# Top-k search in sparse attention: one of two streams of tiles is bisected on ScalarE with sign sums

## The chip, the cores and the metric

One core of one Trainium2 chip. The metric is the device time of one execution in microseconds.

## The reference

Two blocks of a network run one after the other on a sequence of 1024 rows of 1024 features, all in float32. The first block has two layers. In each, a normed and modulated input is projected; one half goes through a spatial gating unit, the other through sparse attention: for every query row an index score against all earlier keys is formed, the 256 best keys are kept, and only these take part in the softmax.

```python
logits = jnp.einsum('bthd,bsd->bths', qib, k_idx) * (IDX_DIM ** -0.5)
score = jnp.einsum('bth,bths->bts', wb, jax.nn.relu(logits)).astype(jnp.float32)
score = jnp.where(causal[None], score, -jnp.inf)
_, idx = lax.top_k(score, top)                     # top = 256
valid = idx <= qpos[None, :, None]
k_sel, v_sel = gather(k, idx), gather(v, idx)
sc = jnp.einsum('bthd,btkd->bthk', qb, k_sel) * attn_scale
p = jax.nn.softmax(jnp.where(valid[:, :, None, :], sc, -jnp.inf), axis=-1)
return jnp.einsum('bthk,btkd->bthd', p, v_sel)
```

The second block has one layer with windowed attention, a gated convolution and a mixture of 32 experts. The change does not touch it.

## The kernel before

The sequence is cut into 8 tiles of 128 rows (tile 0 to tile 7). Rows 0 to 255 keep all their keys, so only tiles 2 to 7 search. Tile i has n = 128 (i + 1) keys.

The search finds, for every one of a tile's 128 rows (one row a partition), the value of the 256th best score. It works on the upper 16 bits of the float scores as signed integers, `up` (L646). One count over `up` says on which side of zero the threshold lies (L648). From it follow `pos`, the rank `K` that is looked for, and the first candidate (L650 to L657). Then a loop of 15 bits (L659 to L666) halves the interval: count how many values reach the candidate (`count`, L605 to L608, one VectorE instruction over n elements with an accumulator output, which the profile shows as TENSOR_SCALAR_CACHE_REDUCE and a DVE_READ_ACCUMULATOR), compare with K (L662, `xb`), move the candidate (L664, `cand`). What the count writes out beside its sum, `junk`, is never read. After the loop `lower` (L690, L695) and `choose` (L702 to L721) take the lower 16 bits and ties into account and write the mask `bias` of the tile.

`select(i)` is a Python generator that does this for tile i: it turns the queries (L544), scores them on TensorE (L629), ScalarE (L632, `rel`) and VectorE (L635, L637), masks the future on GpSimd (L640), searches and chooses. Two streams run interleaved (L762): stream 0 takes tiles 2, 4 and 6, stream 1 tiles 3, 5 and 7 (`z = i % 2` names their small tiles). Each `yield` gives the stream's cost on VectorE and a delay in ns; `bg` and `resume` (L191 to L216) are a planner that emits the next step of the stream that is due first, against a clock of modelled TensorE time, so that the search is interleaved with the dense products. The framework then orders the instructions of each engine by priority with a timing model of its own (`schedule_with_timeline_sim`).

Around the search, in the order of emission: the products of v, u, q, z_a and z_b (`dense_nat`, `dense_T1`; weights arrive as `wraw`, ScalarE makes `whi` at L108, GpSimd `wlo` at L111). The silu of z_b is ScalarE's tanh at L949 and VectorE's L950. L465 and L471 are VectorE's modulation rows, L816 its spatial gating, L507 its part of transposes. `recheck` (L724 to L755) is a branch of VectorE and the DMA queue for rows with many ties; behind it attention (`front`, `back`: L854 to L896) may use the masks, those of tiles 2 to 5 after the second feature block of z_b, those of 6 and 7 later. Attention's Exp is L858 on ScalarE, after VectorE's row maxima (`mx`, L855).

Of the kernel before, what the change touches and what calls it, by code (L numbers as in the profile page):

```python
# [10 lines left out]
FT = mybir.dt.float32  # L11
FR = mybir.dt.float32r
BF = mybir.dt.bfloat16
# [2 lines left out]
U32 = mybir.dt.uint32  # L16
U16 = mybir.dt.uint16
F16 = mybir.dt.float16
AF = mybir.ActivationFunctionType
OP = mybir.AluOpType  # L20
AX = mybir.AxisListType
# [3 lines left out]
S = 1024  # L25
# [15 lines left out]
def tile_hybrid(ctx, tc, I, out):  # L41
    nc = tc.nc
    V, A, G, T = nc.vector, nc.scalar, nc.gpsimd, nc.tensor
# [31 lines left out]
    mhalf = const.tile([128, 16], FT, name="mhalf")  # L75
# [28 lines left out]
    def split(hi, lo, src, which="pool", sub=None):  # L104
        if which == "pool":
            G.tensor_scalar(hi, src, 1.0, 0.0, op0=OP.mult, op1=OP.add)
        elif which == "act":
            A.activation(hi, src, AF.Copy)  # L108
        else:
# [171 lines left out]
    def rms_tile(x, dst, g, scr):  # L281
        ss = small.tile([128, 1], FT, name="ss", bufs=8)
        A.activation(scr, x, AF.Square, accum_out=ss)
        ms = small.tile([128, 1], FT, name="ms", bufs=8)
# [29 lines left out]
    small1 = b1.enter_context(tc.tile_pool(name="small1", bufs=3))  # L314
# [3 lines left out]
    tmp = b1.enter_context(tc.tile_pool(name="tmp", bufs=2))  # L318
# [7 lines left out]
    def rope_tables(after):  # L326
# [14 lines left out]
        for which, q in ((sinT, 0.0), (cosT, 0.25)):  # L341
# [7 lines left out]
            V.tensor_scalar(r, r, -3.1415925, 3.1415925, op0=OP.max, op1=OP.min)  # L349
            A.activation(which, r, AF.Sin)  # L350

# [3 lines left out]
    def silu_c(c8):  # L355
        cc = bank([128, NT], "sm")
        T.transpose(cc, c8, ident[0:NT, 0:NT])
        th = small1.tile([128, NT], FT, name="cct", bufs=1)
        A.activation(th, cc, AF.Tanh, scale=0.5)
        V.scalar_tensor_tensor(th, th, 1.0, cc, op0=OP.add, op1=OP.mult)  # L360
# [12 lines left out]
    def first_h(hT):  # L373
# [8 lines left out]
        def products(c, n, e):  # L382
# [3 lines left out]
            for part in (1, 0):  # L386
# [18 lines left out]
                if e[part] == "m":  # L405
                    A.activation(acc[0:1], pr, AF.Copy)
            return c, n, e, accs

        def use(c, n, e, accs):
# [7 lines left out]
            for cc in range(c, c + n):  # L417
                for b in range(2):
                    ps = bank([128, 4, 128], "tr")
                    for j in range(4):  # L420
# [3 lines left out]
                    y = tmp.tile([128, 512], FT, name="yT", tag="r2", bufs=7)  # L424
                    A.activation(hT[0][:, cc, ts], pv, AF.Identity, scale=mcol[:, 1, cc:cc + 1],
                                 bias=mcol[:, 0, cc:cc + 1])
# [132 lines left out]
    def layer(l, xin, hT=None):  # L559
# [39 lines left out]
        bias, bias_, kept = {}, {}, {}  # L599
        fl = small1.tile([128, 6], BF, name="fl", bufs=1)  # L600
        scd = dram.tile([128, 6, S], FT, name=f"scd{l}")
        junk = tmp.tile([128, S], BF, name="junk", tag="r2", bufs=7)
        headed, scored = set(), set()

        def count(src, thr, op, z):  # L605
            cnt = small1.tile([128, 1], FT, name=f"cnt{z}")
            V.tensor_scalar(junk[:, :src.shape[1]], src, thr, 0.0, op0=op, op1=OP.add, accum_out=cnt)  # L607
            return cnt  # L608

        def select(i):  # L610

            z = i % 2
            n = 128 * (i + 1)
# [31 lines left out]
            up = tmp.tile([128, n], I16, name="up", tag="r2", bufs=7)  # L645
            V.tensor_copy(up, sc.bitcast(I16)[:, 1:2 * n:2])  # L646
            yield 100.0 + .55 * n, False, 0.0, 0.0
            cnt = count(up, 0.0, OP.is_ge, z)  # L648
            pos = small1.tile([128, 1], FT, name=f"pos{z}", bufs=1)
            V.tensor_scalar(pos, cnt, 256.0, None, op0=OP.is_ge)  # L650
            few = small1.tile([128, 1], FT, name=f"few{z}", bufs=1)
# [1 line left out]
            K = small1.tile([128, 1], FT, name=f"K{z}", bufs=1)  # L653
            V.tensor_scalar(K, pos, float(256 - (n - 255)), float(n - 255), op0=OP.mult, op1=OP.add)
            V.tensor_tensor(K, K, few, op=OP.add)
            cand = small1.tile([128, 1], FT, name=f"cand{z}")
            V.tensor_scalar(cand, pos, 32768.0, -16384.0, op0=OP.mult, op1=OP.add)  # L657
            yield 700.0 + .52 * n, False, 0.0, 0.0
            for b in range(14, -1, -1):  # L659
                x = small1.tile([128, 1], FT, name=f"xb{z}")  # L660
                cnt = count(up, cand[:, 0:1], OP.is_ge, z)
                V.tensor_scalar(x, cnt, K[:, 0:1], -float(2 ** b), op0=OP.is_lt, op1=OP.mult)  # L662
                c2 = small1.tile([128, 1], FT, name=f"cand{z}")
                V.scalar_tensor_tensor(c2, x, 2.0 ** (b - 1) if b else 0.0, cand, op0=OP.add, op1=OP.add)  # L664
                cand = c2
                yield 360.0 + .52 * n, False, 0.0, 0.0  # L666

# [30 lines left out]
        def choose(sc, gt, c, cand, z, eq=None, pre=None):  # L698
# [13 lines left out]
            if eq is None:  # L712
                eq = tmp.tile([128, n], BF, name="eq", tag="r2", bufs=7)
                pre = tmp.tile([128, n], F16, name="pre", tag="r2", bufs=7)
            V.tensor_scalar(eq, sc, thr[:, 0:1], None, op0=OP.is_equal)
# [8 lines left out]
        def recheck(tiles):  # L724
# [14 lines left out]
            for arm in tc.Switch({DVE: many, SP: many}, 2):  # L739
                if arm == 1:  # L740
                    for i in tiles:
                        n = 128 * (i + 1)
                        sc, cand = sct[:, :n], kept[i][:, 1:2]
                        up, lw = wt[0][:, 0, :n], wt[0][:, 1, :n].bitcast(U16)
                        eq, pre = wt[1][:, 0, :n].bitcast(BF), wt[1][:, 1, :n].bitcast(F16)
                        nc.sync.dma_start(sc, scd[:, i - 2, :n])
# [10 lines left out]
        def stream(tiles):  # L757
            for i in tiles:
                yield from select(i)
# [331 lines left out]
    hT0 = [big.tile([128, 8, S], FR, name="s32") for _ in range(2)]  # L1091
    rope_tables(first_h(hT0))
    x1 = layer(0, x0, hT0)
    x2 = layer(1, x1)
    b1.close()

# [239 lines left out]
    def gate():  # L1336
        sg = sgpool.tile([128, 2, S], FT, name="sg", tag="sg")

        def ev_g(f, h, ps):
            A.activation(sg[:, f, h * 512:(h + 1) * 512], ps, AF.Tanh, scale=0.5)  # L1340
        dense_T(8, rhs, ev_g)
        return sg
# [3 lines left out]
    sg = gate()  # L1346
# [3 lines left out]
    for br, src in enumerate((convf, attnf)):  # L1350
# [4 lines left out]
        for dc in range(4):  # L1355
            if br or dc:
                sg = gate()
# [58 lines left out]
    pos = keep2.tile([128, NT, 2], FT, name="pos")  # L1416
# [149 lines left out]
    cnt = keep2.tile([128, NE], FT, name="cnt")  # L1566
# [207 lines left out]
```

## Time and profile before

| | us |
|---|---|
| median of 3 runs (lowest, highest) | 2437.85 (2428.63, 2440.24) |
| profiled execution | 2434.67 |
| its span, first to last instruction | 2432.7 |
| first layer's search, first count to attention of tile 2 | about 156 to 503 in the span |
| second layer's search | about 835 to 1160 in the span |

The page gives busy times of the engines (PE is TensorE, DVE VectorE, ACT ScalarE, POOL GpSimd) and cuts the span into 40 slices of 60.8 us; the views below cut it more finely.

### The profile page before, as it was taken

The numbers are of one execution on the slowest core, as the hardware profiler recorded it, in microseconds if no ns is written. First come the engines' busy times: TensorE is split into PE (matmuls) and PEld (weight loads), VectorE is DVE, ScalarE is ACT, GpSimd is POOL, SyncE is SP. The second block draws the span as 40 slices with busy tenths as digits, with TensorE's granted clock in tenths as the row PEclk, the third lists the DMA queues.
The fourth block names the chain that finished last, engine by engine and source line by source line (L and its number), as shares of the span: only waits on it lengthen the run. The fifth ranks groups of instructions, "written<-read, shape, count | busy, mean of one in ns | idle before, by whom it ended". The sixth has DMA issues, their size and how long they took to land. (4 is left out here: it accounts for less than half of the span.)

```text
span 2432.7 us, 36229 instructions
## 1 busy us (share of the span) xinstructions
PE 2165.2 (89%) x13235; PEld 1895.6 (78%) x13235; DVE 1649.2 (68%) x3539; ACT 1065.5 (44%) x1907; POOL 1081.0 (44%) x1006
## 2 busy tenths in 40 slices
PE   5998898699989979986999899999999897899996
PEld 5897786577779978964878698888888676888875
DVE  8779898977774688897778427872010335798875
ACT  4333333455642333334646335652121212678775
POOL 4654465447745652745455245533233512232221
PEclk9999999789999989987999999999999998999998
DMA  7522112311114111123120211113121164999995
GB/s 233 186 80 82 47 31 77 97 61 58 53 38 135 48 36 47 41 72 96 49 84 23 52 44 36 31 31 81 48 64 45 50 238 165 305 346 336 333 335 153
DMA packets 146508, 265.50 MB, mean 109 GB/s; under 512 B 23672, under 2 KB 100880, under 8 KB 134016
## 3 DMA queue, kind: packets, MB, share of 16 engines
q1 hardware_dynamic: 139136, 241.99, 30.2%
q0 software_dynamic: 7168, 20.98, 4.0%
q8 instruction: 105, 1.72, 0.3%
q14 instruction: 99, 0.81, 0.1%
HBM read 228.83 MB, written 38.29 MB: 110 GB/s over the span
## 5 line engine op out<-in xcount | busy, mean ns | idle before, releaser
L111 POOL TENSOR_TENSOR wlo<-wraw,whi 128x512 fp32r<-128x512 f32 (+1 forms) x188 | 253.6, 1350 | 490.3 <-ACT whi L108 472.8
L101 PE MATMUL big<-wlo,s 128*128 128x256 f32 (+1 forms) x1536 | 440.0, 288 | 11.0 <-POOL wlo L111 11.0
L100 PE MATMUL big<-whi,s 128*128 128x256 f32 (+1 forms) x1536 | 437.8, 289 | 11.7 <-ACT s L506 9.3
L102 PE MATMUL big<-whi,s 128*128 128x256 f32 (+1 forms) x1536 | 440.1, 288 | 0.0
L101 PEld LDWEIGHTS big<-wlo,s 128*128 128x128 f32 x1536 | 298.7, 195 | 16.1 <-POOL wlo L111 13.4
L100 PEld LDWEIGHTS big<-whi,s 128*128 128x128 f32 x1536 | 296.2, 194 | 19.1 <-ACT s L506 11.9
L108 ACT ACTIVATE whi<-wraw 128x512 fp32r<-128x512 f32 (+1 forms) x188 | 117.8, 628 | 417.4 <-PE big L102 140.9
L102 PEld LDWEIGHTS big<-whi,s 128*128 128x128 f32 x1536 | 298.2, 194 | 2.9 <-issue 0.9
L111 DVE TENSOR_TENSOR ew<-s,ew 128x1024 fp32r<-128x1024 f32 x138 | 162.8, 1221 | 35.0 <-ACT ew L108 33.7
L607 DVE TENSOR_SCALAR_CACHE_REDUCE junk<-up,cand 128x512 bf16<-128x512 int16 (+5 forms) x192 | 179.8, 937 | 1.4
L637 DVE SCALAR_TENSOR_TENSOR s<-rel,widx,s 128x384 f32<-128x384 f32 (+3 forms) x140 | 130.5, 956 | 51.0 <-ACT rel L632 50.5
L632 ACT ACTIVATE rel<-sm 128x384 f32<-128x384 f32 (+3 forms) x160 | 80.9, 524 | 161.9 <-PE sm L629 104.4
L100 PE MATMUL half<-s,whi 128*128 128x512 f32 x320 | 133.1, 417 | 18.0 <-DVE s L950 14.7
L108 ACT ACTIVATE ew<-s 128x1024 fp32r<-128x1024 f32 x138 | 137.8, 1049 | 25.3 <-PE sm L102 16.3
L100 PE MATMUL sm<-ew,xT 128*96 128x256 f32 x512 | 146.6, 286 | 2.0 <-ACT xT L1621 2.0
L102 PE MATMUL sm<-ew,xT 128*96 128x256 f32 x512 | 147.3, 288 | 0.6 <-DVE xT L1622 0.6
L101 PE MATMUL sm<-ew,xT 128*96 128x256 f32 x512 | 145.3, 284 | 0.8 <-DVE ew L111 0.7
L101 PE MATMUL half<-s,whi 128*128 128x512 f32 x320 | 131.2, 410 | 0.0
L102 PE MATMUL half<-s,wlo 128*128 128x512 f32 x320 | 129.8, 409 | 0.3 <-POOL wlo L111 0.3
L1659 POOL DMA_INDIRECT out_dram<-yt,yi x32 | 60.1, 1878 | 149.9 <-DMA out_dram<-yt,yi 86.5
L862 POOL TENSOR_SCALAR Z<-Z,rc 128x128 f32<-128x128 f32 (+7 forms) x88 | 63.4, 733 | 108.9 <-DVE rc L860 66.4
L629 PE MATMUL sm<-kist,qT 128*128 128x384 f32 (+3 forms) x320 | 91.2, 376 | 14.4 <-ACT rel L632 13.0
(624 smaller groups left out, 6118.0 us busy)
## 6 DMA issues: line engine op xcount, KB each, us to landing
wraw<-in_w_in_dram SPq DMA_DIRECT2D x164, 256.0 KB
adaw<-in_w_ada_dram SPq DMA_DIRECT2D x48, 512.0 KB
s<-in_w_gate_e_dram SPq DMA_DIRECT2D x23, 1024.0 KB
s<-in_w_up_e_dram SPq DMA_DIRECT2D x23, 1024.0 KB
s<-in_w_down_e_dram SPq DMA_DIRECT2D x23, 1024.0 KB
X<-in_w_gate_e_dram SPq DMA_DIRECT2D x9, 1024.0 KB
X<-in_w_up_e_dram SPq DMA_DIRECT2D x9, 1024.0 KB
X<-in_w_down_e_dram SPq DMA_DIRECT2D x9, 1024.0 KB
```

Source lines behind the costliest of these rows:

```text
L100: T.matmul(o, lh, rh, start=start, stop=False, skip_group_check=True)
L101: T.matmul(o, lh, rl, start=False, stop=False, skip_group_check=True)
L102: T.matmul(o, ll, rh, start=False, stop=stop, skip_group_check=True)
L108: A.activation(hi, src, AF.Copy)
L111: return (sub or V).tensor_tensor(lo, src, hi.bitcast(FT), op=OP.subtract)
L607: V.tensor_scalar(junk[:, :src.shape[1]], src, thr, 0.0, op0=op, op1=OP.add, accum_out=cnt)
L629: T.matmul(ps[:, :w_], qT[g][:, j, :], kist[a][:, p * w_:(p + 1) * w_], start=a == 0, stop=a == 1)
L632: A.activation(rel[:, :w_], ps[:, :w_], AF.Relu, scale=0.125)
L637: V.scalar_tensor_tensor(d, rel[:, :w_], widx[:, i, h:h + 1], d, op0=OP.mult, op1=OP.add)
L862: G.tensor_scalar(P[hh][:, :n], P[hh][:, :n], rc[:, hh:hh + 1], 1.0, op0=OP.mult, op1=OP.mult)
L1659: return G.indirect_dma_start(out=out, out_offset=bass.IndirectOffsetOnAxis(ap=ycol, axis=0), in_=yt, in_offset=None, bounds_check=S + SL ...
```

## The change

For tiles 3, 5 and 7 the first count and the 15 bits move from VectorE to ScalarE. A count becomes one activation, Sign(up - candidate + 0.5), with an accumulator output: its sum is (number above) minus (number below). A second Sign over one column says whether the count reaches K, and an Identity over one column moves the (negated) candidate. A few scalings of one column around the loop stay on VectorE. These steps charge the planner no VectorE time and a delay of 800 + 0.85 n ns a bit. For tiles 2, 4 and 6 the candidate's move (L664) becomes a tensor_scalar with the old candidate as a per-partition scalar. `junk` becomes two halves of 8-bit integers in the same bytes, one for VectorE's counts and one for ScalarE's.

```diff
--- before.py
+++ after.py
@@ -16,6 +16,7 @@
 U32 = mybir.dt.uint32
 U16 = mybir.dt.uint16
 F16 = mybir.dt.float16
+I8 = mybir.dt.int8
 AF = mybir.ActivationFunctionType
 OP = mybir.AluOpType
 AX = mybir.AxisListType
@@ -599,8 +600,36 @@
         bias, bias_, kept = {}, {}, {}
         fl = small1.tile([128, 6], BF, name="fl", bufs=1)
         scd = dram.tile([128, 6, S], FT, name=f"scd{l}")
-        junk = tmp.tile([128, S], BF, name="junk", tag="r2", bufs=7)
+        junk8 = tmp.tile([128, 2, S], I8, name="junk", tag="r2", bufs=7)
+        junk = junk8[:, 0]
         headed, scored = set(), set()
+
+        junk2 = junk8[:, 1]
+
+        def count_act(up, off, scale=1.0):
+
+            sg = small1.tile([128, 1], FT, name="xb1")
+            A.activation(junk2[:, :up.shape[1]], up, AF.Sign, bias=off, scale=scale, accum_out=sg)
+            return sg
+
+        def bisect_act(up, K, pos, n):
+
+            kb = small1.tile([128, 1], FT, name="few1", bufs=1)
+            V.tensor_scalar(kb, K, -2.0, float(n + 1), op0=OP.mult, op1=OP.add)
+            nc_ = small1.tile([128, 1], FT, name="cand1")
+            V.tensor_scalar(nc_, pos, -32768.0, 16384.5, op0=OP.mult, op1=OP.add)
+            for b in range(14, -1, -1):
+                sg = count_act(up, nc_[:, 0:1])
+                s_ = small1.tile([128, 1], FT, name="cnt1")
+                A.activation(s_, sg, AF.Sign, bias=kb[:, 0:1])
+                if b:
+                    n2 = small1.tile([128, 1], FT, name="cand1")
+                    A.activation(n2, s_, AF.Identity, scale=-2.0 ** (b - 1), bias=nc_[:, 0:1])
+                    nc_ = n2
+                yield 0.0, False, 800.0 + .85 * n, 0.0
+            cand = small1.tile([128, 1], FT, name="cand1")
+            V.tensor_scalar(cand, s_, 0.5, nc_[:, 0:1], op0=OP.mult, op1=OP.subtract)
+            return cand
 
         def count(src, thr, op, z):
             cnt = small1.tile([128, 1], FT, name=f"cnt{z}")
@@ -645,7 +674,12 @@
             up = tmp.tile([128, n], I16, name="up", tag="r2", bufs=7)
             V.tensor_copy(up, sc.bitcast(I16)[:, 1:2 * n:2])
             yield 100.0 + .55 * n, False, 0.0, 0.0
-            cnt = count(up, 0.0, OP.is_ge, z)
+            if z:
+                sg = count_act(up, mhalf[:, 0:1], -1.0)
+                cnt = small1.tile([128, 1], FT, name=f"cnt{z}")
+                V.tensor_scalar(cnt, sg, -0.5, 0.5 * n, op0=OP.mult, op1=OP.add)
+            else:
+                cnt = count(up, 0.0, OP.is_ge, z)
             pos = small1.tile([128, 1], FT, name=f"pos{z}", bufs=1)
             V.tensor_scalar(pos, cnt, 256.0, None, op0=OP.is_ge)
             few = small1.tile([128, 1], FT, name=f"few{z}", bufs=1)
@@ -653,15 +687,18 @@
             K = small1.tile([128, 1], FT, name=f"K{z}", bufs=1)
             V.tensor_scalar(K, pos, float(256 - (n - 255)), float(n - 255), op0=OP.mult, op1=OP.add)
             V.tensor_tensor(K, K, few, op=OP.add)
-            cand = small1.tile([128, 1], FT, name=f"cand{z}")
-            V.tensor_scalar(cand, pos, 32768.0, -16384.0, op0=OP.mult, op1=OP.add)
-            yield 700.0 + .52 * n, False, 0.0, 0.0
-            for b in range(14, -1, -1):
+            if not z:
+                cand = small1.tile([128, 1], FT, name=f"cand{z}")
+                V.tensor_scalar(cand, pos, 32768.0, -16384.0, op0=OP.mult, op1=OP.add)
+            yield 700.0 + (0.0 if z else .52 * n), False, 0.0, 0.0
+            if z:
+                cand = yield from bisect_act(up, K, pos, n)
+            for b in () if z else range(14, -1, -1):
                 x = small1.tile([128, 1], FT, name=f"xb{z}")
                 cnt = count(up, cand[:, 0:1], OP.is_ge, z)
                 V.tensor_scalar(x, cnt, K[:, 0:1], -float(2 ** b), op0=OP.is_lt, op1=OP.mult)
                 c2 = small1.tile([128, 1], FT, name=f"cand{z}")
-                V.scalar_tensor_tensor(c2, x, 2.0 ** (b - 1) if b else 0.0, cand, op0=OP.add, op1=OP.add)
+                V.tensor_scalar(c2, x, 2.0 ** (b - 1) if b else 0.0, cand[:, 0:1], op0=OP.add, op1=OP.add)
                 cand = c2
                 yield 360.0 + .52 * n, False, 0.0, 0.0
 
```

## Rows read from the trace of the kernel before

**Rows 1.** The page: busy time, share of the span and instructions of each engine, and the 40 slices of TensorE and VectorE in tenths.
```profile
PE 2165.2 (89%) x13235; PEld 1895.6 (78%) x13235; DVE 1649.2 (68%) x3539; ACT 1065.5 (44%) x1907; POOL 1081.0 (44%) x1006
...
PE   5998898699989979986999899999999897899996
...
DVE  8779898977774688897778427872010335798875
```

**Rows 2.** Busy time of each engine in stretches of the two searches (stretch in us from the start of the span: its length, then the busy time and instructions of TensorE, its weight loads, VectorE, ScalarE and GpSimd; then the granted TensorE clock as a share of full speed, the DMA share and GB/s). Six stretches for each layer: tiles 2 and 3 bisected, between, tiles 4 and 5, between, tiles 6 and 7, the tail.
```profile
156.00:216.00 60.00, 55.36 (x444) 52.98 (x442) 59.14 (x205) 17.61 (x29) 15.33 (x12) 1.00 0.37 105
216.00:270.00 54.00, 44.49 (x278) 40.71 (x279) 46.43 (x56) 19.66 (x41) 35.82 (x23) 0.81 0.23 64
270.00:345.00 75.00, 64.22 (x467) 59.91 (x466) 73.34 (x199) 20.33 (x38) 32.81 (x35) 0.98 0.16 42
345.00:384.00 39.00, 35.14 (x247) 33.25 (x247) 30.23 (x38) 17.94 (x33) 36.13 (x35) 0.96 0.14 40
384.00:456.00 72.00, 59.89 (x263) 47.92 (x261) 70.57 (x185) 24.24 (x56) 23.16 (x28) 0.91 0.25 77
456.00:503.00 47.00, 24.34 (x93) 17.64 (x91) 38.12 (x88) 24.31 (x57) 30.08 (x28) 0.60 0.29 91
835.00:893.00 58.00, 44.27 (x328) 42.72 (x327) 57.67 (x192) 20.07 (x36) 32.84 (x25) 0.85 0.12 36
893.00:938.00 45.00, 45.00 (x356) 44.91 (x357) 29.67 (x64) 19.87 (x41) 8.27 (x7) 1.00 0.18 50
938.00:993.00 55.00, 50.07 (x381) 48.06 (x380) 54.38 (x153) 14.07 (x25) 31.37 (x33) 1.00 0.15 42
993.00:1040.00 47.00, 42.94 (x298) 40.99 (x297) 37.70 (x63) 19.96 (x35) 34.70 (x35) 0.93 0.14 39
1040.00:1115.00 75.00, 63.72 (x292) 50.69 (x290) 73.10 (x183) 24.45 (x59) 24.98 (x30) 0.91 0.24 74
1115.00:1160.00 45.00, 21.75 (x87) 16.68 (x86) 30.63 (x74) 25.07 (x56) 28.66 (x28) 0.62 0.34 101
```

**Rows 3.** Who TensorE waited for from 156 to 503 us, longest in total first (instruction and line that waited, who released it: us in total, times, longest).
```profile
PE half L100 <- DVE s L950: 11.3, 3, 6.8
PE sm L629 <- ACT rel L632: 8.0, 6, 3.5
PE sm L854 <- DVE qT L544: 5.5, 1, 5.5
PE tr L538 <- DVE wml L507: 5.3, 1, 5.3
PE sm L469 <- DVE ada L465: 5.1, 1, 5.1
...
PE sm L100 <- DVE bt L471: 2.4, 1, 2.4
...
PE sm L100 <- DVE xb L662: 2.0, 2, 1.7
```

**Rows 4.** Groups of VectorE instructions from 156 to 503 us, shapes kept apart (line, operation, tiles, shapes, count; busy us, mean ns of one; idle before).
```profile
L664 DVE SCALAR_TENSOR_TENSOR cand<-xb,cand 128x1 f32<-128x1 f32 x90 | 26.8, 298 | 0.5
L607 DVE TENSOR_SCALAR_CACHE_REDUCE junk<-up,cand 128x1024 bf16<-128x1024 int16 x16 | 20.3, 1271 | 0.1
...
L662 DVE TENSOR_SCALAR xb<-cnt,K 128x1 f32<-128x1 f32 x90 | 18.6, 207 | 0.3
...
L607 DVE TENSOR_SCALAR_CACHE_REDUCE junk<-up,cand 128x768 bf16<-128x768 int16 x16 | 16.0, 1001 | 0.0
...
L607 DVE TENSOR_SCALAR_CACHE_REDUCE junk<-up,cand 128x512 bf16<-128x512 int16 x16 | 11.7, 733 | 0.0
...
L607 DVE DVE_READ_ACCUMULATOR junk<-up,cand 128x1 f32 x96 | 7.8, 81 | 0.0
```

**Rows 5.** Groups of ScalarE instructions of the whole span, shapes kept apart: the Exp of attention with a pointer bias and an accumulator output, its accumulator read, a two-column activation without pointers, and the table loads ahead of Silu (L936) and Exp (L858).
```profile
L858 ACT ACTIVATION_READ_ACCUMULATOR Z<-Z,mx 128x1 f32 x88 | 16.6, 189 | 0.0
...
L858 ACT ACTIVATE Z<-Z,mx 128x1024 f32<-128x1024 f32 x8 | 9.2, 1153 | 1.9 <-DVE mx L855 1.9
...
L858 ACT ACTIVATE Z<-Z,mx 128x768 f32<-128x768 f32 x8 | 7.4, 930 | 2.9 <-DVE mx L855 2.9
...
L858 ACT ACTIVATE Z<-Z,mx 128x128 f32<-128x128 f32 x16 | 6.4, 399 | 42.6 <-DVE mx L855 42.6
L1229 ACT ACTIVATE mx<-mx 128x2 f32<-128x2 f32 x32 | 6.3, 195 | 8.3 <-DVE mx L1228 8.1
...
L858 ACT ACTIVATE Z<-Z,mx 128x512 f32<-128x512 f32 x8 | 5.7, 717 | 0.3 <-DVE mx L855 0.3
...
L936 ACT ACT_TABLE_LOAD x2 | 2.6, 1283 | 0.0
L858 ACT ACT_TABLE_LOAD x2 | 2.6, 1283 | 0.0
```

**Rows 6.** VectorE in order of time: the first and the last count of tile 7 in the first layer (start us, us, engine, line, operation).
```profile
412.36 1.27 DVE L607 TENSOR_SCALAR_CACHE_REDUCE junk<-up,cand 128x1024 bf16<-128x1024 int16 x1
...
464.84 1.28 DVE L607 TENSOR_SCALAR_CACHE_REDUCE junk<-up,cand 128x1024 bf16<-128x1024 int16 x1
```

**Rows 7.** Who ScalarE waited for from 156 to 503 us: the row of the Exp.
```profile
ACT Z L858 <- DVE mx L855: 32.1, 12, 7.7
```

**Rows 8.** TensorE in order of time: one matmul of z_b at 1.2 GHz, and one of the same shape at 2.4 GHz (start us, us).
```profile
409.33 0.63 PE L102 MATMUL half<-s,wlo 128*128 128x512 f32 x1
...
415.86 0.40 PE L102 MATMUL half<-s,wlo 128*128 128x512 f32 x1
```

## Prediction

> **What bounds the kernel now.** I read the page first: TensorE is busy 89% of the span and VectorE 68%, ScalarE only 44% [rows 1]. By the averages TensorE is the bound. The slices say where it is not: VectorE's row of tenths stands at 7 to 9 while the two top-k searches run, and TensorE's row dips to 6 at the end of each [rows 1]. So next I cut the two search stages into stretches [rows 2]. In the first layer VectorE is busy 59.1 of 60, 73.3 of 75 and 70.6 of 72 us in the three stretches where tiles 2 and 3, 4 and 5, 6 and 7 are bisected, and the second layer repeats this (57.7 of 58, 54.4 of 55, 73.1 of 75). There VectorE is full, and TensorE loses time. Over the six stretches of the first layer TensorE is busy 283.4 of 347 us, so it idles 63.6; over those of the second 267.8 of 325, 57.2 idle.
>
> The waits of TensorE say for whom it idles: for a VectorE result that stands in VectorE's queue among the counts. L950 (the silu of z_b) costs 11.3 us, L507 5.3, L465 5.1, L471 2.4, L662 2.0 [rows 3], together 26.1; another 8.0 is ScalarE's rel of the scoring. The tails (456 to 503 and 1115 to 1160, when the last tile's mask is made and the attention of tiles 2 and 3 starts) hold 22.7 and 23.3 us of idle TensorE [rows 2]. Last, the granted clock is 0.60 and 0.62 in the tails and 0.81 to 1.00 elsewhere [rows 2]: idle TensorE also falls from 2.4 to 1.2 GHz, where one matmul takes 0.63 instead of 0.40 us [rows 8].
>
> **The change part by part.** *VectorE, removed for tiles 3, 5, 7.* Per layer 16 counts a tile go (one for the sign, 15 bits): 16 x (0.733 + 1.001 + 1.271) = 48.1 us; 48 accumulator reads at 0.081 = 3.9; 45 of L662 at 0.207 = 9.3; 45 of L664 at 0.298 = 13.4 [rows 4]. That is 74.7. Added are four small scalings a tile (cnt, kb, the first and the last cand) against the one cand that goes: 9 x 0.207 = 1.9.
>
> *VectorE, tiles 2, 4, 6.* L664 turns from a form with two tensor inputs into one with one tensor and a per-partition scalar, the form of L662. Mean 298 against 207 ns [rows 4]: 45 x 0.091 = 4.1 us a layer saved. Bounds: nothing, and 10 us, were the form as short as the accumulator read (81 ns). The count now writes 8-bit junk. No row shows that output; the counts cost 1.05 ns an element ((1271 - 733) / 512 [rows 4]). I take nothing; were it twice as slow per element, the 45 counts left would cost some 38 us a layer more and half of the relief would be gone. Net relief taken: 77 us a layer, of 318 and 283 that VectorE is busy in the two stages [rows 2].
>
> *ScalarE, added.* One bit is a Sign over n elements with a pointer bias and an accumulator read, a Sign of one column and an Identity of one column. The nearest row to the first is the Exp of the attention, which also has a pointer bias and an accumulator: 717, 930 and 1153 ns for 512, 768 and 1024 columns, and 189 for the read [rows 5]. A column of one lies between L1229 (195 ns, no pointer) and the 128-column Exp (399 ns) [rows 5]; taking 0.85 ns a column off the latter ((1153 - 717) / 512) leaves 290, which I use. A bit is then 1.49, 1.69, 1.92 us, a tile 22, 25, 29 us, with the first counts 80 us a layer (bounds 71 and 89). ScalarE goes from 124 to 204 of 347 us in the first stage: not a bound.
>
> The Trainium skill speaks against this: "ScalarE: Activation LUTs", section Rules for kernel authors, wants simple elementwise work on VectorE, which it puts at up to three times as fast. By that a 1024-column count would take 3.8 us on ScalarE and tile 7's chain nearly 70 us. The trace disagrees for this operation: 1271 ns on VectorE [rows 4], 1153 on ScalarE [rows 5].
>
> *The chain of tile 7.* Its 15 bits and the last count stand from 412.4 to 466.1 on VectorE [rows 6], 53.7 us, though one bit by itself is 1.27 + 0.08 + 0.21 + 0.16 = 1.7 us: the rest is other work in the queue. On ScalarE the bits are 29 us; ScalarE is busy 24.2 of 72 us there [rows 2], so stretched by 1 / (1 - 0.34) the chain takes 44, and it starts earlier since VectorE scores sooner. Tile 6 keeps VectorE to itself at the same time. What is late next: the z_b products, which keep TensorE until 456, and then the branch of recheck, which VectorE takes only behind the masks that stand in front of it.
>
> *The queues.* No transfer is moved. Instructions behind a Sign on ScalarE wait up to 1.2 us: the rel of the scoring, the whi halves of the weights, the evacuations, all of which TensorE waits for. There are 254 ScalarE instructions in the stage [rows 2], and the new work holds ScalarE 80 / 347 = 23% of it. Half a count, 0.47 us, x 0.23 x 254 = 27 us a layer if each were on TensorE's path; double buffers cover most, as rel ends only 8.0 us of TensorE's idle time now [rows 3]. I take a quarter, 7 us. The planner's yields change too: stream 1 charges VectorE nothing and is paced by 800 + 0.85 n ns a bit, about what I get above for a bit (1.24 to 1.67 against 1.49 to 1.92), so the search is emitted no later.
>
> *Sum.* (a) Of the 26.1 us of VectorE-ended waits outside the tail two thirds go, since VectorE falls from full to about 60%: 17; the second layer by its idle time (57.2 / 63.6): 16. (b) The tails are chains of latency, but begin earlier and with z_b products still to fill TensorE: half, 11 + 12. (c) Clock: busy time x (1 - clock) over the stretches of [rows 2] is 26 + 24 us lost to 1.2 GHz; a third comes back with the idle time, 16. (d) ScalarE's queue: -14. Together 58 us. The profiled execution took 2434.67 us (span 2432.7), so 2377; it lies 3 us under the median of the runs, so I say 2378.
>
> **The rivals.** *The tail stays.* The masks are ready sooner, but the branch and the first attention units set the tail (the wait on L544 behind the branch is 5.5 us [rows 3]). Then (b) is nothing and (c) half: 33 + 8 - 14 = 27, 2410. For it: that longest wait of the tail stands behind the branch, not behind a count. Against: tile 7's last count ends at 466 [rows 6], inside the tail.
>
> *The wait moves to ScalarE.* All 27 us a layer of (d) count: 58 + 14 - 54 = 18 faster; if the tail stays too, 2435 to 2440. No change. For it: ScalarE feeds TensorE with everything. Against: it is 34% busy in that stretch.
>
> *Slower: the bits stand behind Exps.* ScalarE runs in order, and the Exps of the first attention units wait 32.1 us for VectorE's maxima in the first stage [rows 7]. A bit queued behind such an Exp waits with it. With all of it in tile 7's chain it takes 29 + 18 + 32 = 79 us against 53.7 now: the tail comes 25 us later in each layer, 2435 + 50 - 33 + 14 = 2466. It decides once over 7 us of these waits fall between bits and VectorE's relief shortens none of them; but the maxima wait in the very queue that is relieved.
>
> *Slower: function tables.* Loads of 1.283 us stand ahead of the first Silu and the first Exp of a layer [rows 5]; Relu, Copy and Identity bring none. If Sign were not in the table of Exp, every turn from a bit to an Exp and back would cost 2.6 us; with 15 turns in tile 7's chain 38 us a layer, the end 28 us later: 2435 + 56 - 33 = 2458. Beside this stands the Trainium skill, "ScalarE: Activation LUTs", section Table sets: it wants calls grouped by table set, and lists cheap functions as part of every set without naming Sign in that list; no row here shows Sign.
>
> **How the numbers follow.** Forecast 0.62 (its own range 2330 to 2410); the tail stays 0.15; the wait moves to ScalarE 0.10; behind Exps 0.09; tables 0.04. The first two are faster: 0.77. The third is the same: 0.10. The last two are slower: 0.13. About 0.5%, 12 us, is what the runs can tell from no change. The low end takes all of (a), the whole of both tails and half of (c), without (d): 50 + 46 + 25 = 121, 2314; I cut it to 2322. The high end, 2440, takes in the unchanged case and leaves out the two slower ones.
>
> **What would show it.** Right: VectorE's busy time down by some 150 us and ScalarE's up by some 160; a Sign of 1024 columns near 1.15 us; VectorE at 60 to 75% in the six stretches; the L950, L507 and L465 waits nearly gone; tails at a higher clock; no more table loads than before. Wrong: counts with 8-bit output above 1.3 us for 896 columns; new waits of TensorE on ScalarE above 20 us a layer; bits more than 3 us apart with an Exp waiting between them; the end of tile 7's search no earlier relative to the z_b products.

## The result: 0.8% slower

The changed kernel takes 2456.2 us (median; 2447.1 to 2460.6) against 2437.8 for the kernel before: a ratio of 1.0078, 95% interval 1.0062 to 1.0094. I had forecast 2378, with a range of 2322 to 2440, and given slower a chance of 0.13.

The page of the changed kernel (busy time, and the rows of TensorE, VectorE and ScalarE in 40 slices), against [rows 1]:

```profile
PE 2175.8 (89%) x13235; PEld 1898.2 (77%) x13235; DVE 1532.6 (62%) x3185; ACT 1199.9 (49%) x2273; POOL 1063.6 (43%) x1006
...
PE   5999598689988988985999899999999888899986
...
DVE  8677967377864587763868517873010234798875
ACT  4355362854642464538546424663121111778774
```

The work moved as meant: VectorE is 117 us less busy and ScalarE 134 more, TensorE's work is the same 13235 matmuls (10.6 us longer busy). Yet TensorE's row falls to 5 where it stood at 8 in the fifth slice (246 to 307 us, in the first search), and to 5 where it stood at 6 in the nineteenth (1105 to 1167 us, the end of the second).

To place the loss I cut each layer at three events that every kernel here has: the first `up` of the search, the start of the last tanh of z_b (L949, here L986), and the first use of an output projection (L1028, here L1065). Between the first two lies what I call the head, in which the search runs beside dense products; between the last two the tail, in which the search ends and attention begins. The same view as [rows 2], for the kernel before (head, tail, head, tail):

```profile
156.80:457.80 301.00, 258.95 (x1689) 234.36 (x1687) 281.04 (x683) 100.80 (x198) 144.17 (x131) 0.93 0.23 67
457.80:518.30 60.50, 37.68 (x160) 28.00 (x161) 48.68 (x114) 34.81 (x81) 34.08 (x35) 0.69 0.33 106
829.80:1118.50 288.70, 251.79 (x1688) 232.58 (x1686) 260.19 (x679) 103.24 (x205) 133.75 (x131) 0.93 0.18 51
1118.50:1173.00 54.50, 34.06 (x153) 26.62 (x154) 38.37 (x93) 32.56 (x75) 32.75 (x35) 0.69 0.36 112
```

And for the changed kernel:

```profile
160.20:450.70 290.50, 251.90 (x1658) 226.15 (x1656) 220.48 (x494) 142.60 (x317) 137.32 (x126) 0.92 0.23 69
450.70:529.70 79.00, 47.26 (x193) 36.84 (x193) 46.41 (x124) 58.83 (x145) 33.17 (x42) 0.61 0.26 83
844.80:1116.70 271.90, 244.94 (x1649) 226.47 (x1647) 202.66 (x468) 143.48 (x315) 130.60 (x124) 0.93 0.19 55
1116.70:1197.00 80.30, 46.21 (x193) 34.20 (x193) 46.07 (x124) 60.03 (x149) 33.07 (x42) 0.66 0.23 75
```

The heads gain 10.5 and 16.8 us, the tails lose 18.5 and 25.8; 3.4 us more are lost ahead of the first head and 3.6 between the layers, and the rest of the span shifts by the sum, 24. About half of a tail's loss (9.6 and 12.2 us of TensorE's busy time) is products that now run there (193 matmuls where there were 160 and 153), at a granted clock of 0.61 and 0.66 where it was 0.69; the rest is idle TensorE.

In the tail tile 7's bits are now a chain on ScalarE. The Signs of its 15 bits (the line's instructions from 430 to 500 us; durations min/median/max, first and last start), and VectorE's wait for the last of them:

```profile
L612 ACT ACTIVATE junk<-up,cand x15: 1132/1147/1150, 440.5 to 491.1; 128x1024 int8<-128x1024 int16 x15
```
```profile
DVE cand L631 <- ACT cnt L624: 5.4, 1, 5.4
```

TensorE's waits from 156 to 530 us (who waited, for whom: total, times, longest):

```profile
PE sm L101 <- DVE e L713: 14.0, 1, 14.0
PE sm L891 <- DVE mx L892: 12.1, 2, 11.0
PE sm L658 <- ACT rel L661: 9.7, 7, 2.7
...
PE half L101 <- DVE s L987: 5.0, 1, 5.0
```

The z_b wait of [rows 3] fell from 11.3 to 5.0 us, the way that was forecast, but the longest is new, and the second has more than doubled. In the kernel before, the same stretch had for it:

```profile
PE sm L854 <- DVE mx L855: 5.2, 4, 2.4
```

That wait, for attention's first maxima (L892, before L855), is the tail's; the 14.0 us belong to the head. VectorE in that stretch (start, duration):

```profile
285.81 0.21 DVE L699 TENSOR_SCALAR xb<-cnt,K 128x1 f32<-128x1 f32 x1
286.06 0.21 DVE L701 TENSOR_SCALAR cand<-xb,cand 128x1 f32<-128x1 f32 x1
286.31 0.88 DVE L636 TENSOR_SCALAR_CACHE_REDUCE junk<-up,cand 128x640 int8<-128x640 int16 x1
...
295.59 0.75 DVE L853 SCALAR_TENSOR_TENSOR X<-sm,bs,X 128x512 f32<-128x512 f32 x1
296.26 0.22 DVE L713 SCALAR_TENSOR_TENSOR e<-rank,K,m 128x8 f32<-128x8 f32 x1
```
```profile
296.49 0.77 PE L101 MATMUL sm<-vs,wmh 128*128 128x512 f32 x1 [13.96 <-DVE e L713]
```

From 279 to 291 us VectorE does nothing but the bits of tile 4, one every 1.42 us. L853, which empties the `sm` bank that the spatial gating's next products need, stands behind them and behind four more us of tile 4's next steps and tile 5's scoring. (The profile names `e`, L713, which ends 0.14 us after L853, as the releaser.) In the kernel before the bits of tiles 4 and 5 alternate at this place and the same instruction (L816 there) is let in between:

```profile
291.57 0.86 DVE L607 TENSOR_SCALAR_CACHE_REDUCE junk<-up,cand 128x640 bf16<-128x640 int16 x1
...
292.44 0.74 DVE L816 SCALAR_TENSOR_TENSOR X<-sm,bs,X 128x512 f32<-128x512 f32 x1
...
293.22 1.00 DVE L607 TENSOR_SCALAR_CACHE_REDUCE junk<-up,cand 128x768 bf16<-128x768 int16 x1
```

### The profile page after: what moved, and what is told of

It reads as the page before. It is cut to its first block, busy times and chain, and to the rows that moved or that the text cites. A ratio compares the mean times of both kernels' runs of the same rounds, so it can differ in the third digit from the quotient of the medians.

```text
span 2456.2 us, 36272 instructions
## 1 busy us (share of the span) xinstructions
PE 2175.8 (89%) x13235; PEld 1898.2 (77%) x13235; DVE 1532.6 (62%) x3185; ACT 1199.9 (49%) x2273; POOL 1063.6 (43%) x1006
## 5 line engine op out<-in xcount | busy, mean ns | idle before, releaser
L102 PEld LDWEIGHTS big<-wlo,s 128*128 128x128 f32 x1536 | 295.5, 193 | 19.0 <-POOL wlo L112 16.8
L101 PEld LDWEIGHTS big<-whi,s 128*128 128x128 f32 x1536 | 292.8, 192 | 20.4 <-ACT s L507 11.0
L103 PEld LDWEIGHTS big<-whi,s 128*128 128x128 f32 x1536 | 295.4, 193 | 1.2
L666 DVE SCALAR_TENSOR_TENSOR s<-rel,widx,s 128x384 f32<-128x384 f32 (+3 forms) x140 | 118.4, 867 | 91.5 <-ACT rel L661 91.2
L1696 POOL DMA_INDIRECT out_dram<-yt,yi x32 | 53.5, 1673 | 131.7 <-DMA out_dram<-yt,yi 43.8
L101 PE MATMUL big<-s,whi 128*128 128x512 f32 x256 | 101.2, 395 | 0.3 <-DVE convf L1349 0.3
L102 PE MATMUL big<-s,whi 128*128 128x512 f32 x256 | 101.1, 395 | 0.0
```

The costliest lines, as they stand in the source:

```text
L101: T.matmul(o, lh, rh, start=start, stop=False, skip_group_check=True)
L102: T.matmul(o, lh, rl, start=False, stop=False, skip_group_check=True)
L103: T.matmul(o, ll, rh, start=False, stop=stop, skip_group_check=True)
L666: V.scalar_tensor_tensor(d, rel[:, :w_], widx[:, i, h:h + 1], d, op0=OP.mult, op1=OP.add)
L1696: return G.indirect_dma_start(out=out, out_offset=bass.IndirectOffsetOnAxis(ap=ycol, axis=0), in_=yt, in_offset=None, bounds_check=S + SL ...
```

## The experiments

Three theories were set against each other. A: tile 7's bits are one long serial chain on a busy ScalarE at the end of the search. B, later called D: bits on ScalarE disturb its other work, whatever the tile. C: the planner's pace changed the order of emission, and the loss is one of order. Each kernel was timed in five rounds beside the kernel before, whose median lay at 2436 to 2438 us.

**The scalar form alone.** The kernel before, with

```
- V.scalar_tensor_tensor(c2, x, 2.0 ** (b - 1) if b else 0.0, cand, op0=OP.add, op1=OP.add)
+ V.tensor_scalar(c2, x, 2.0 ** (b - 1) if b else 0.0, cand[:, 0:1], op0=OP.add, op1=OP.add)
```

> One part alone: the kernel before, with the candidate's move of all six tiles in the form with a per-partition scalar, and nothing on ScalarE. All theories of the loss lie in the ScalarE search, so all expect no loss here. By the rows of the two traces (298 ns before, 0.207 us for such a form) VectorE is relieved by 90 x 0.091 = 8 us a layer, on a VectorE that is full there: 2422 to 2438 us. If the loss came from this part, the time would be 2445 or more.

2416.8 us, ratio 0.9926 (0.9912 to 0.9940): 19 us faster, below the 2422 to 2438 that were expected. The loss is not here; the rest of the change (the bits on ScalarE, their pace, the 8-bit `junk`) costs 39 us on top of this. L664 over the whole span, before and in this kernel:

```profile
L664 DVE SCALAR_TENSOR_TENSOR cand<-xb,cand 128x1 f32<-128x1 f32 x180 | 60.6, 337 | 1.6
```
```profile
L664 DVE TENSOR_SCALAR cand<-xb,cand 128x1 f32<-128x1 f32 x180 | 37.7, 210 | 1.5
```

**Which tiles.** In the changed kernel the condition `if z` became `if i in (3, 5)`, and in a second kernel `if i in (7,)`; the other tiles stay on VectorE in the scalar form.

> The changed kernel with tile 7 back on VectorE; only tiles 3 and 5 are bisected on ScalarE. Theory A (the long pole: tile 7's bits end late because they are one serial chain on a ScalarE that other work fills at the end of the search): the tail's loss of 18 to 26 us a layer goes and the 10 to 15 us gained ahead of it stay, so 2405 to 2425 us, and the wait of TensorE for the first attention's maxima (12.1 and 12.6 us) shrinks. Theory B (any ScalarE bits disturb the evacuations, whichever tile they belong to): two thirds of the loss stay, about 2450 us. Theory C (the planner emits stream 1 too late): tile 5's delay still pushes tile 7 back, so its first count comes later than 412 us and the time stays at 2440 or more.

> Only tile 7 is bisected on ScalarE, tiles 3 and 5 on VectorE. Theory A: the relief ahead of the tail is missing, and the tail is as in the changed kernel or a little better, as tile 7 starts earlier than with tile 5 in its stream on ScalarE: 2445 to 2475 us. Theory B: a third of the bits, a third of the loss: about 2444 us. Theory C: tile 7's scoring begins about when it did before (up at 408 us), so the tail is as long as before and the time is 2438 us or less.

Tiles 3 and 5: 2443.1 us, ratio 1.0027 (1.0015 to 1.0039), 26 above the scalar form alone. Tile 7: 2419.4 us, 0.9926 (0.9911 to 0.9941), the same within noise. These times are the reverse of theory A: with tile 7 back on VectorE most of the loss stays, and tile 7 alone costs next to nothing. B, which asked for 2444, doesn't fit tile 7's figure either. Theory C has both times right, but not tile 7's tail: it was to be as long as before, and it is 82 and 83 us against 59 and 53 in the scalar form. The heads are 25 and 29 us shorter, so that the sum comes out at nothing (table below).

**The planner's delay of a bit.** From 800 + 0.85 n ns to half, to 0.7 and to a quarter of it:

```
- yield 0.0, False, 800.0 + .85 * n, 0.0
+ yield 0.0, False, 400.0 + .42 * n, 0.0      (0.7: 560.0 + .6 * n; a quarter: 200.0 + .21 * n)
```

> The changed kernel with half the planner's delay a bit (400 + 0.42 n ns in place of 800 + 0.85 n). Theory C: the bits and then tile 7's scoring are emitted earlier, tile 7's up is made well before 435 us (by 420 or less), the tail begins earlier, and the time falls by 10 to 20 us a layer, to 2415 to 2436 us. Theory A: the chain is bound by ScalarE's queue, not by the order of emission; tile 7's search ends within 5 us of 500 us and the time stays at 2445 to 2460 us.

> The changed kernel with 0.7 of its delay (560 + 0.6 n ns a bit). Theory C: between half (2399) and full (2456) the time follows how late tile 7 starts: 2405 to 2435 us, tile 7's up between 385 and 435 us. If the half delay is a lucky order and no point of a slope, the time can come out anywhere, at 2440 us or more too.

> The changed kernel with a quarter of its delay a bit (200 + 0.21 n ns). Theory C: what half the delay gave back (57 us) goes on a little or has reached its end, where the bits are bound by ScalarE and VectorE and no longer by emission: 2380 to 2405 us. Theory D: bits emitted still closer together stand in front of the evacuations in ScalarE's queue, and the time rises above 2410 us.

Half: 2398.8 us, 0.9840 (0.9826 to 0.9855). 0.7: 2423.1 us, 0.9942 (0.9927 to 0.9956). A quarter: 2491.3 us, 1.0233 (1.0214 to 1.0253). No instruction is added or taken away between these, and the time moves over 92 us. Down to the half it follows theory C, at the half beyond its numbers. The quarter's loss is against C; D had asked for it, with a time above 2410 us. The quarter's waits, of VectorE and of TensorE from 156 to 560 us:

```profile
DVE cand L631 <- ACT cnt L624: 49.1, 3, 16.8
```
```profile
PE sm L470 <- DVE ada L466: 36.8, 1, 36.8
```

With a ScalarE bit charged as a quarter of its delay, the instruction that reads the last bit (L631) comes far too early in VectorE's queue; VectorE stands there 49 us in three waits, and the modulation row that TensorE wants stands behind one of them. In the changed kernel these waits were 9.3 us. None of the theories had this wait, but D's reason is there beside it: in the second layer nine bits of tile 5 stand back to back on ScalarE (964 to 979 us) ahead of a `rel` that TensorE waits 15.4 us for.

**The pace without any Sign.** The scalar form alone, with only the changed kernel's yields for tiles 3, 5 and 7 (no VectorE cost, 800 + 0.85 n ns); and its counterpart, the scalar form with half the cost of every bit (180 + 0.26 n ns).

> No Sign at all: the kernel with the candidate's move in the scalar form (2417 us), in which only the planner's pace of tiles 3, 5 and 7 is taken from the changed kernel (no VectorE cost, 800 + 0.85 n ns of delay a bit). Theory C (the pace emits tile 7 too late): tile 7's up comes behind some 2180 and 4810 of the dense products, as in the changed kernel, instead of 2091 and 4704, and the time rises to 2435 to 2475 us. Theory D (the bits on ScalarE's queue cost it): 2410 to 2425 us.

> No Sign: the kernel with the scalar form (2417 us), with half the modelled cost of a VectorE bit (180 + 0.26 n ns), so that all six tiles are emitted earlier. If the gain of the half delay is one of pace alone, this gets it too: 2395 to 2410 us. If it needs the relief of VectorE, the bits only stand longer in VectorE's queue ahead of what TensorE waits for: 2417 us or more.

Pace alone: 2452.6 us, 1.0068 (1.0054 to 1.0082). Not one bit is on ScalarE, and the time is 36 us above the scalar form, nearly the changed kernel's 39. The loss isn't in the same place, though: against the scalar form the heads here are 18.5 and 3.9 us longer and the tails 1.9 and 7.1, while in the changed kernel the heads are 1.4 and 10.2 us shorter and the tails 19.6 and 27.1 longer. So the pace alone is enough for a loss of this size, but that the two are nearly equal is in part chance. The head has the changed kernel's long wait again (`e` L676 here is L713 there):

```profile
PE sm L629 <- ACT rel L632: 17.0, 10, 5.7
PE sm L100 <- DVE e L676: 13.0, 1, 13.0
```

Tile 7's `up` is not as late as theory C had it, though (2108 and 4724 products, in the table below). Half the cost: 2434.0 us, 0.9995 (0.9984 to 1.0007), 17 slower than with the full cost. So early emission as such doesn't give the gain of the half delay; with all bits on VectorE it costs time.

**Shorter Signs.** Each Sign over 128 columns, with a constant for the threshold that is then not found, and with the flag for `recheck` set so high that its branch is not taken, at the full delay and at the half.

```
- A.activation(junk2[:, :up.shape[1]], up, AF.Sign, bias=off, scale=scale, accum_out=sg)
+ A.activation(junk2[:, :128], up[:, :128], AF.Sign, bias=off, scale=scale, accum_out=sg)
```

> The changed kernel with its full delay, but each Sign counts 128 columns instead of 512 to 1024; the threshold that tiles 3, 5 and 7 find is left out with that (a constant stands in its place), and the steps after it stay. ScalarE is relieved of some 65 us a layer, and a bit of tile 7 needs about 1.2 instead of 1.9 us. Theory C: the order of emission is the same, the start of tile 7 stays late, and the time falls by 15 us at most: 2440 to 2456 us. Theory D: with the work on ScalarE its cost goes: 2400 to 2430 us.

> Half the delay (2399 us), with Signs over 128 columns; the threshold of tiles 3, 5 and 7 is left out with that, as in the short Signs at the full delay (2430 us, 26 us under the changed kernel). It measures what the length of the bits on ScalarE costs where the pace is good. Theory C: emission is by the planner's clock and the bits have room: 2385 to 2400 us. Theory D: the bits' length is worth the same 26 us or more here: 2375 us or less.

2430.4 us at the full delay (0.9978, 0.9964 to 0.9991), 2383.5 at the half (0.9780, 0.9767 to 0.9793): 26 and 15 us less. At the full delay that is more than theory C allowed and at the edge of what D asked; at the half it is 2 us more than C allowed and 9 short of what D asked. The length of the chain has a price of its own, beside that of the order.

**The old pace.** The changed kernel, bits on ScalarE, with the yields of the kernel before.

```
- yield 0.0, False, 800.0 + .85 * n, 0.0
+ yield 360.0 + .52 * n, False, 0.0, 0.0
```

> The changed kernel, with the bits of tiles 3, 5 and 7 on ScalarE, but with the planner told what the kernel before told it (360 + 0.52 n ns of VectorE time a bit for all tiles), so that the two streams alternate as before. Theory C: with the order of emission given back (tile 7 behind some 2091 and 4704 of the products), the move itself shows its worth: VectorE is relieved of some 75 us a layer against the kernel in the scalar form alone (2417 us), so 2380 to 2410 us. Theory D: the bits on ScalarE cost as much as they relieve, or more: 2415 to 2455 us.

2386.8 us, 0.9795 (0.9782 to 0.9807): 51 us faster than the kernel before and 69 faster than the change as made. Head, tail, head, tail:

```profile
161.70:432.80 271.10, 251.94 (x1696) 230.39 (x1694) 231.19 (x521) 163.52 (x371) 146.05 (x134) 0.96 0.25 75
432.80:491.10 58.30, 36.47 (x154) 27.75 (x155) 40.39 (x98) 38.23 (x91) 33.82 (x35) 0.68 0.34 110
802.00:1058.50 256.50, 241.97 (x1682) 225.37 (x1681) 203.53 (x493) 156.86 (x348) 137.11 (x130) 0.98 0.20 58
1058.50:1126.00 67.50, 36.55 (x159) 26.83 (x159) 39.12 (x101) 47.05 (x115) 30.29 (x36) 0.70 0.27 88
```

**Which half of the pace.** The old yields differ from the new in two ways: the odd stream's own delay, and that its bits hold back the even stream. Here the odd stream keeps 800 + 0.85 n, and only the even stream (tiles 2, 4 and 6) gets a delay as well.

```
- yield 360.0 + .52 * n, False, 0.0, 0.0
+ yield 360.0 + .52 * n, False, 360.0 + .52 * n, 0.0
```

> The changed kernel with its full delay a bit for tiles 3, 5 and 7; only tiles 2, 4 and 6 get a delay too, as long as their modelled cost (360 + 0.52 n ns), so that they no longer run ahead of the other stream. Two readings of the pace stand against each other. C1 (the even stream runs ahead, since nothing of the other is charged to VectorE any more, and with it the order of all that follows): the order is nearly that of the old pace (2387 us), so 2385 to 2405 us. C2 (the delay of 800 + 0.85 n ns is itself too long for the odd stream): it stands unchanged, tile 7 is as late as before, and the time stays at 2440 to 2460 us.

2383.7 us, 0.9788 (0.9768 to 0.9807): 72 us less than the change as made, by one yield, and with the old pace the best of the kernels that find the threshold. Head, tail, head, tail, and VectorE among the bits of tile 4, where L853 is let in between again:

```profile
156.90:423.70 266.80, 251.33 (x1679) 226.72 (x1677) 234.00 (x513) 158.67 (x356) 142.78 (x131) 0.96 0.26 76
423.70:487.70 64.00, 40.69 (x173) 30.25 (x174) 43.04 (x108) 44.53 (x106) 35.33 (x38) 0.68 0.32 101
800.90:1062.50 261.60, 245.67 (x1682) 228.46 (x1681) 206.19 (x494) 164.54 (x368) 137.71 (x130) 0.96 0.20 57
1062.50:1122.60 60.10, 36.49 (x158) 27.58 (x159) 41.53 (x98) 39.29 (x95) 32.76 (x36) 0.69 0.32 99
```
```profile
279.28 0.87 DVE L636 TENSOR_SCALAR_CACHE_REDUCE junk<-up,cand 128x640 int8<-128x640 int16 x1
...
280.25 0.75 DVE L853 SCALAR_TENSOR_TENSOR X<-sm,bs,X 128x512 f32<-128x512 f32 x1
...
281.41 0.88 DVE L636 TENSOR_SCALAR_CACHE_REDUCE junk<-up,cand 128x640 int8<-128x640 int16 x1
```

The delay I had looked at can stay as it is; that the even stream was let run ahead is what cost the time.

## Why the prediction was wrong

**The step that failed** is in the part on the queues: "stream 1 charges VectorE nothing and is paced by 800 + 0.85 n ns a bit ... so the search is emitted no later". I checked the pace of the stream that was moved and not of the one that stayed, and so put the change of order at nothing; the runs put it at 69 and 72 us (the old pace and the slowed even stream against the change as made). The planner's line `s_[1] = dve[0] = max(dve[0], s_[1], now[0]) + cost` keeps one VectorE clock for both. Before, each bit of one stream pushed the other back, and a stream got a bit in about 2 x (360 + 0.52 n). With nothing charged for stream 1, stream 0 is emitted a bit every 360 + 0.52 n = 693 ns (n = 640), while the trace has one every 1.42 us. Tiles 4 and 6 then run far ahead, with their bits in blocks on VectorE.

What became of the order, behind the planner and the framework's own ordering, can be counted in the traces: how many of the 9840 products of `mm3` start on TensorE before a tile's `up` is made, beside the lengths of head and tail in us (first layer / second layer):

| kernel | products before tile 6 | before tile 7 | head | tail |
|---|---|---|---|---|
| before | 1994 / 4538 | 2091 / 4704 | 301.0 / 288.7 | 60.5 / 54.5 |
| scalar form alone | 1994 / 4539 | 2091 / 4704 | 291.9 / 282.1 | 59.4 / 53.2 |
| changed | 1790 / 4390 | 2179 / 4810 | 290.5 / 271.9 | 79.0 / 80.3 |
| tiles 3 and 5 | 1789 / 4388 | 2179 / 4810 | 290.2 / 273.7 | 73.4 / 72.2 |
| tile 7 alone | 2088 / 4656 | 2185 / 4820 | 266.7 / 253.4 | 81.8 / 83.0 |
| pace alone, no Sign | 1786 / 4372 | 2108 / 4724 | 310.4 / 286.0 | 61.3 / 60.3 |
| half the cost, no Sign | 1861 / 4537 | 2111 / 4675 | 305.9 / 274.1 | 64.7 / 56.1 |
| short Signs, full delay | 1764 / 4374 | 2179 / 4802 | 286.1 / 268.7 | 70.4 / 70.9 |
| short Signs, half the delay | 1897 / 4626 | 1970 / 4656 | 291.8 / 263.6 | 43.9 / 53.1 |
| 0.7 of the delay | 1896 / 4576 | 2152 / 4843 | 278.9 / 254.8 | 69.3 / 86.9 |
| half the delay | 1862 / 4690 | 1946 / 4710 | 295.8 / 263.1 | 45.4 / 65.9 |
| a quarter of the delay | 2080 / 4580 | 1717 / 4066 | 331.8 / 320.4 | 50.8 / 45.3 |
| old pace | 1987 / 4562 | 2097 / 4762 | 271.1 / 256.5 | 58.3 / 67.5 |
| even stream slowed | 1960 / 4562 | 2114 / 4713 | 266.8 / 261.6 | 64.0 / 60.1 |

The surest pair is the change as made and the slowed even stream, one yield apart: in the first layer tile 6 goes back from 1790 to 1960 products and tile 7 comes forward from 2179 to 2114 (in the second 4390 to 4562 and 4810 to 4713), the heads are 24 and 10 us shorter and the tails 15 and 20. Over all kernels the tail goes with tile 7's place: 44 to 68 us where it stands at 2114 and 4762 or earlier, 69 to 87 where it stands at 2152 and 4802 or later. At the same late place it is 73 and 72 us with tile 7 on VectorE, 79 and 80 on ScalarE, 70 and 71 with short Signs: the chain's length is the smaller part. A late tile 7 also takes work out of the head, so heads compare only at a like place of tile 7. They do between tile 7 alone and the change as made: 267 and 253 us where the even stream doesn't run ahead, 290 and 272 where it does.

Why tile 7 stands so late in the changed kernel is open in part. With the pace alone it is only 17 and 20 products late, and nearly the whole loss is in the head. One thing that I had put at nothing is not excluded, the 8-bit `junk`. In the first layer the kernel with tile 7 alone on ScalarE has, up to tile 7's `up`, the instructions and the yields of the scalar form but for the 8-bit output of the counts; its own Signs and pace come behind. Yet tile 6 stands at 2088 there and not at 1994, tile 7 at 2185 and not at 2091. The 8-bit output costs VectorE no time (below), so it would have moved the order, perhaps through the framework's timing model. No run has it alone, so this is not shown. That tile 6 and tile 7 go back to near their old places when the even stream is slowed, with the 8-bit output still there, is shown.

**Point by point.** The sizes of single instructions were right. The changed kernel's groups (shapes apart; busy, mean ns):

```profile
L612 ACT ACTIVATE junk<-up,cand 128x1024 int8<-128x1024 int16 x30 | 34.3, 1142 | 0.5
...
L624 ACT ACTIVATE cnt<-xb,few 128x1 f32<-128x1 f32 x90 | 26.1, 290 | 3.9 <-DVE kept L717 2.4
...
L627 ACT ACTIVATE cand<-cnt,cand 128x1 f32<-128x1 f32 x84 | 24.5, 291 | 1.8
...
L973 ACT ACT_TABLE_LOAD x2 | 2.6, 1283 | 0.0
L895 ACT ACT_TABLE_LOAD x2 | 2.6, 1283 | 0.0
```
```profile
L636 DVE TENSOR_SCALAR_CACHE_REDUCE junk<-up,cand 128x896 int8<-128x896 int16 x16 | 18.3, 1144 | 0.5
```

And the count over 896 columns in the kernel before:

```profile
L607 DVE TENSOR_SCALAR_CACHE_REDUCE junk<-up,cand 128x896 bf16<-128x896 int16 x32 | 36.6, 1142 | 0.6
```

1142 ns against the 1153 taken from Exp, 290 and 291 for the one-column steps against 290 worked out, no table load more, and VectorE's counts with 8-bit output as fast as with 16-bit (1144 against 1142 ns for 896 columns, under the 1.3 us that was to be the sign). The rival of the tables is out. VectorE's busy time fell by 117 where I said 150 and ScalarE's rose by 134 for 160: I had added up durations, and the records of neighbouring instructions overlap (added up, VectorE's fell by 158 and ScalarE's rose by 157).

(a) and (c), the waits and the clock of the heads: in the changed kernel 27 us; with the order kept (the old pace) 62, as TensorE's idle time in the heads falls from 79.0 to 33.7 us and its busy time by another 16.8. I had 33 + 16 - 14 = 35. (d), the queue of ScalarE: with the old pace TensorE waits 3.6 us for `rel` in the first head against 8.0 before, so of the 7 us a layer nothing is seen there.

(b), half of the tails' idle time, is wrong even with the old pace: the tails come out at 58.3 and 67.5 us against 60.5 and 54.5. Tile 7's chain does what I said of it there: its bits begin at 398.1, 14 us earlier than before, and take 47 us (51 in the second layer). But the products end 25 us earlier as well (432.8 against 457.8), so less is left to run beside the end of the search; I had moved the one and left the other where it was. In the changed kernel "the chain takes 44, and it starts earlier" fails too: the 15 bits take 52 us (440.5 to 492.7), no less than the same 15 on VectorE (412.4 to 464.8; the 54 of the prediction have one count more), and begin 28 us later, between 16 copies of output weights (9.7 us) and 16 Exps (7.1 us) of the first attention units.

The forecast of 2378 lies within 9 us of the old pace and 6 of the slowed even stream: the whole is worth what I said where the order is kept, but that the sum fits so well is in part luck. Its terms were off both ways: heads 62 for the 35 of (a), (c) and (d), tails a loss of 11 for the gain of 23 of (b). And 19 of the 51 us are the scalar form's, which I had counted at 8 us of VectorE's time and no more; ScalarE's part is worth some 30. Of the signs for it, the sizes and the table loads came true, and the L950, L507 and L465 waits fell to 5.0, 0.8 and nothing; the tails' clock fell where it was to rise. Of the signs against it, one came true: tile 7's search ends no earlier relative to the z_b products. Its MAX8 stood 12 us behind the last tanh before and stands 49 behind it now. The rival "behind Exps" had 25 us a layer in the tail, and the tails lost 18.5 and 25.8, but not for its reason: the bits are 3.6 us apart, with Exps between them, but no wait of ScalarE for VectorE's maxima falls into tile 7's chain.

## What to carry to other kernels

When work moves to another engine and a planner, a cost model or a hand-written order was fed by it, recompute the pace of the work that stays, not only of the work that moves; then run the old order with the new engine once, since that tells the worth of the move from the worth of the order (here 51 us gained, the scalar form's 19 among them, and 69 given back). Here the end of the search followed its place in the engines' queues first and the speed of its chain second. A chain charged as much quicker than it is cost time too, since the instruction that reads its result stood in VectorE's queue ahead of other work (49 us in three waits). And a loss of the same size is no proof of the same cause: compare stage by stage, as with the pace alone.

## What the runs showed of the hardware

The small candidate move, which I had priced at 4.1 us of VectorE's time a layer for three tiles, was worth more than its mean in [rows 4] let me see. As an instruction with two tensor inputs of one column it took from 114 to 1244 ns, with one tensor and a per-partition scalar from 184 to 219 (the line's durations min/median/max, before and with the scalar form):

```profile
L664 DVE SCALAR_TENSOR_TENSOR cand<-xb,cand x180: 114/159/1244, 163.6 to 1115.6; 128x1 f32<-128x1 f32 x180
```
```profile
L664 DVE TENSOR_SCALAR cand<-xb,cand x180: 184/210/219, 166.6 to 1102.5; 128x1 f32<-128x1 f32 x180
```

Split by what GpSimd did at the time, the 106 during which it was idle for half of the time or more took 153 ns on average (161 at most) and the 74 beside a busy GpSimd 600. The same split of the scalar form gives 209 and 210 ns, and a split by ScalarE's work in the kernel before gives 341 and 328. The Trainium skill, "GPSIMD Engine Reference", section 8. Key points, says that GpSimd shares its SBUF interfaces with VectorE and contends with VectorE instructions that have two SBUF inputs; the trace agrees (600 ns against 153). The mean of 298 ns that I used was an average of these two cases, and the form that is slower by itself (210 against 153) was 19 us faster in the kernel.
